# Local attention on one core: look-ahead of three items instead of two, a fourth buffer of v, and class-order copies on VectorE

## The chip, the core and the metric

The kernel runs on one core of a Trainium2 chip. A core has a matrix engine (TensorE, PE in the profile, with its weight loads apart as PEld), a vector engine (VectorE, DVE), a scalar engine (ScalarE, ACT), a general engine (GpSimd, POOL) and a queue engine that here only issues DMA transfers (SyncE, SP). Each engine takes its own instructions strictly in the order in which the program gives them, and waits on semaphores for the work of others. The metric is the device time of one launch in microseconds (us). PEclk in the profile is the clock granted to TensorE: 1.00 is 2.4 GHz and 0.50 is 1.2 GHz; a value between them is a stretch with some of each.

## The reference

Two blocks follow each other on 1024 tokens of width 1024. The first (gated linear attention, pooling, a mixture of experts) is not touched. The second computes a short gated convolution and eight heads of dilated local attention, and multiplies both by `w_out_2`. What matters here is the attention:

```python
DILATED_CONFIGS = ((128, 1), (512, 4), (2048, 16))      # (window, dilation)
q = rmsnorm_2(q.reshape(b, s, 8, 64), q_norm_w)
k = rmsnorm_2(k.reshape(b, s, 8, 64), k_norm_w)
for window, dilation in DILATED_CONFIGS:
    # queries and keys are split into `dilation` residue classes, swept in blocks of 128 queries
    logits = einsum('bhnqd,bhnkd->bhnqk', qr, kblk) * 64 ** -0.5
    logits = where(mask, logits + bias, -1e30)
    m = max(logits); p = exp(logits - m); denom = sum(p)
    o_i = einsum('bhnqk,bhnkd->bhnqd', p, vblk) / denom;  lse_i = m + log(denom)
mix = softmax(stack(lses), axis=0)
o = einsum('gbsh,gbshd->bshd', mix, stack(outs))
y_attn = o.reshape(b, s, 512) * silu(z_attn)
x = x + concatenate([y_conv, y_attn]) @ w_out
```

## The kernel before

The attention runs over four pairs of heads. A pair has 12 items: four of dilation 4 (configuration 1), four of dilation 16 (configuration 2), four of dilation 1 (configuration 0), in this order; `stream` lists the 48 items. One round of the loop at L1683 is a step g, and each engine gets its instructions in the order in which a step writes them:

- `load_values` of item g+2: SP issues the DMA of its block of v into a tile `vt` (L1454 to L1464, three buffers).
- `powers` of item g+2: TensorE makes the scores (L1500), VectorE adds the bias and takes the row's extreme value (L1506), ScalarE takes the exponential (L1508). The result is the tile `sb`.
- `turn_powers` of item g+1: TensorE transposes `sb` (L1526); the result is copied from PSUM to `pt`, one half by ScalarE (L1528), one by VectorE (L1530).
- `weigh` of item g: TensorE multiplies `pt` with `vt` (L1559), ScalarE copies the result to `og` (L1561, L1564 or L1566, by configuration).
- On some steps `next_part`: twelve matmuls of a product with `w_out_2` (L161 to L163), which needs nothing of the attention.
- `late.step()`: work put off by a number of steps. One such part is `mix_weights` (L1580 to L1594) and its `spread`: TensorE transposes the mixing weights (L1599), ScalarE copies them (L1601), SP writes them to DRAM as `sw_d` (L1603) and reads them back six times, broadcast (`zb`, L1607, 256 KB each). Another is `close_heads` (L1617 to L1621): POOL and VectorE multiply the three outputs of a pair by `zb` and add them. `ship_stats` sends row statistics to DRAM and back (`st_d`, L1574 to L1578).

Configurations 1 and 2 need queries and keys in class order. `by_class` makes these copies: `qd` and `kd` (L1487), 128x1024 fp32 each, read with steps of 4 or 8 elements (16 or 32 bytes). Configuration 2's are written behind the powers of item (1,1) of a pair, those of configuration 1 of the next pair behind the powers of item (0,1). A pair of numbers like (0,1) is configuration and item. So each pair has four copies, 16 in all; two are made before the loop.

Tiles come from pools of a fixed number of buffers: 26 of 4 KB under the name "blk" (`sb`, `pt`, `og`, `qd`, `kd`, `zb`, parts of `w_out_2`), six "tmp", four "wr" (raw weights), eight banks of PSUM.

Of the kernel before, what the change touches and what calls it, by code (L numbers as in the profile page):

```python
# [12 lines left out]
F32 = mybir.dt.float32  # L13
# [7 lines left out]
P = 128  # L21
# [44 lines left out]
def first_then_second_block(ctx: ExitStack, tc: tile.TileContext, a: dict, out: bass.AP):  # L66
    nc = tc.nc
    V, A, G, PE, SY = nc.vector, nc.scalar, nc.gpsimd, nc.tensor, nc.sync
# [7 lines left out]
    NTMP = 6  # L76
# [8 lines left out]
    def blk(name, shape=(P, 2, 512), dtype=F32):  # L85
        return B.tile(list(shape), dtype, name=name, tag="blk", bufs=NBLK)

    def psum(shape, name="ps"):
        t = PS.tile([P, 512], F32, name=name, tag="ps")
        n = int(np.prod(shape[1:]))  # L90
        v = t[: shape[0], :n]
        if len(shape) == 3:
            v = v.rearrange("p (a b) -> p a b", a=shape[1])
        elif len(shape) == 4:
            v = v.rearrange("p (a b c) -> p a b c", a=shape[1], b=shape[2])
        return v
# [194 lines left out]
    W = first.enter_context(tc.tile_pool(name="first", bufs=1))  # L291
# [836 lines left out]
    with tc.For_i(0, end_reg, 1):  # L1128
# [48 lines left out]
        for i, w in enumerate((wg, wu)):  # L1177
            src = w[bass.ds(e_reg, 1)].rearrange("o (p k) n -> p (o k) n", p=P)
# [15 lines left out]
        src = wd[bass.ds(e_reg, 1)].rearrange("o (p k) n -> p (o k) n", p=P)  # L1194
# [18 lines left out]
    W = att.enter_context(tc.tile_pool(name="attn", bufs=1))  # L1213
# [219 lines left out]
    hd = {}  # L1433
    def begin_heads(hp):
        s = hd[hp] = {}
        b14 = W.tile([P, 2, 2, 256], F32, name="b14", tag="b14", bufs=2)
        b16 = W.tile([P, 2, P], F32, name="b16", tag="b16", bufs=2)
        for h in range(2):
            for c in range(2):
                SY.dma_start(b14[:, c, h, :], dram_ap(skew_d, ((2 * hp + h) * 3 + c) * SKEW + P - 1, [[NSK - 1, P], [1, 256]]))  # L1440
            SY.dma_start(b16[:, h, :], dram_ap(skew_d, ((2 * hp + h) * 3 + 2) * SKEW + P - 1, [[NSK - 1, P], [1, P]]))
        s["bias"] = b14, b16
        s["tok"] = W.tile([P, 3, 8, 2, 2], F32, name="tok", tag="tok", bufs=2)
        s["st"] = [s["tok"][:, 0]] + [W.tile([P, 8, 2, 2], F32, name=f"st{c}", tag=f"st{c}", bufs=2) for c in (1, 2)]
        s["og"], s["sb"], s["pt"], s["v"] = {}, {}, {}, {}
        s["qk"] = {0: (qT[hp], kT[hp])}

    def load_values(hp, cfg, pr):
        c0 = hp * P
        v = hd[hp]["v"][cfg, pr] = W.tile([P, 3, P], F32, name="vt", tag="vt", bufs=3)  # L1450
        if cfg == 0:
            lo, hi = 256 * pr - 64, 256 * pr + 320
            if pr == 0:
                SY.dma_start(v[:64, 0, :], v_d[:64, c0:c0 + P])  # L1454
                lo += P
            if pr == 3:
                SY.dma_start(v[64:, 2, :], v_d[960:, c0:c0 + P])
                hi -= P
            k0 = (lo + 64 - 256 * pr) // P
            SY.dma_start(v[:, k0:k0 + (hi - lo) // P, :], v_d[lo:hi, c0:c0 + P].rearrange("(c p) n -> p c n", p=P))  # L1460
        elif cfg == 1:
            SY.dma_start(v[:, :2, :], v_d.rearrange("(b p r) n -> p b r n", p=P, r=4)[:, :, pr, c0:c0 + P])
        else:
            SY.dma_start(v[:, :2, :], v_d.rearrange("(p i) n -> p i n", i=8)[:, 2 * pr:2 * pr + 2, c0:c0 + P])  # L1464
# [17 lines left out]
    def by_class(hp, cfg):  # L1482
        n = DILS[1] if cfg == 1 else 8
        both = []
        for name, src in (("qd", qT[hp]), ("kd", kT[hp])):
            dst = blk(name, (P, n, T // n))
            G.tensor_copy(dst, src.rearrange("p (l r) -> p r l", r=n))  # L1487
            both.append(dst.rearrange("p r l -> p (r l)"))
        hd[hp]["qk"][cfg] = both

    def powers(hp, cfg, pr):
        s = hd[hp]
        qs, ks = s["qk"][cfg]
        b14, b16 = s["bias"]
        sp = [psum((P, 2, 256)) for _ in range(2)]
        sb = s["sb"][cfg, pr] = blk("sb")
        for i, (qc, kc, boff, n) in enumerate(units_of(cfg, pr)):
            for h in range(2):
                r = slice(64 * h, 64 * h + 64)
                PE.matmul(sp[h][:, i, :n], qs[r, qc], ks[r, kc], start=True, stop=True)  # L1500
        for i, (qc, kc, boff, n) in enumerate(units_of(cfg, pr)):
            for h in range(2):
                bias = b16[:, h, :] if cfg == 2 else b14[:, cfg, h, boff:boff + n]
                stat = s["st"][cfg][:, 2 * pr + i, h, :]
                p = sb[:, h, STEP[cfg] * i:STEP[cfg] * i + n]
                s_min = V.tensor_tensor_reduce(out=p, in0=sp[h][:, i, :n], in1=bias, scale=1.0, scalar=3.0e38,  # L1506
                                               op0=OP.add, op1=OP.min, accum_out=stat[:, 0:1])
                s_exp = A.activation(p, p, AF.Exp, bias=stat[:, 0:1], scale=-1.0, accum_out=stat[:, 1:2])  # L1508
                newest[:] = [s_min.ins, s_exp.ins]
# [70 lines left out]
    def mix_weights(hp):  # L1580
        s = hd[hp]
        tok = s["tok"]
        mn = W.tile([P, 8, 2], F32, name="mn", tag="mn", bufs=2)
        V.tensor_tensor(mn, tok[:, 0, :, :, 0], tok[:, 1, :, :, 0], op=OP.min)
        V.tensor_tensor(mn, mn, tok[:, 2, :, :, 0], op=OP.min)
        sg = W.tile([P, 3, 8, 2], F32, name="sg3", tag="sg3", bufs=2)
        V.tensor_sub(sg, mn[:, None].to_broadcast([P, 3, 8, 2]), tok[:, :, :, :, 0])
        A.activation(sg, sg, AF.Exp)
        zz = W.tile([P, 3, 8, 2], F32, name="zz", tag="zz", bufs=2)
        V.tensor_mul(zz, sg, tok[:, :, :, :, 1])  # L1590
        V.tensor_add(mn, zz[:, 0], zz[:, 1])
        V.tensor_add(mn, mn, zz[:, 2])
        V.reciprocal(mn, mn)
        sw = W.tile([P, 3, 2, 8], F32, name="sw", tag="sw", bufs=2)  # L1594
        V.tensor_mul(sw.rearrange("p c h b -> p c b h"), sg, mn[:, None].to_broadcast([P, 3, 8, 2]))

        def spread():
            ps = psum((48, P))
            PE.transpose(ps, sw.rearrange("p c h b -> p (c h b)"), ident)  # L1599
            swT = W.tile([48, P], F32, name="swT", tag="swT", bufs=1)  # L1600
            A.copy(swT, ps)  # L1601
            w_d = tc.dram_tile([6, T], F32, name=f"sw_d{hp}")
            SY.dma_start(w_d.rearrange("c (b p) -> (c b) p", p=P), swT)  # L1603
            s["zb"] = [blk("zb", (P, T)) for _ in range(3)]
            for cfg in range(3):
                for h in range(2):
                    SY.dma_start(s["zb"][cfg][64 * h:64 * h + 64, :], w_d[2 * cfg + h:2 * cfg + h + 1, :].to_broadcast([64, T]))  # L1607

        late.at(SPREAD, spread)
# [72 lines left out]

    stream = [(hp,) + it for hp in range(4) for it in items]  # L1683
    NS = len(stream)
    for g in range(-2, NS):
        if g + 2 < NS:
            hp, cfg, pr = stream[g + 2]
            if g == -2:
                begin_heads(hp)
                by_class(hp, cfg)  # L1690
            load_values(hp, cfg, pr)
            powers(hp, cfg, pr)
            if (cfg, pr) == (1, 1):
                by_class(hp, 2)
            elif (cfg, pr) == (0, 1) and hp < 3:
                begin_heads(hp + 1)
                by_class(hp + 1, 1)
            if cfg and pr == 3:
                late.at(2, lambda hp=hp, cfg=cfg: ship_stats(hp, cfg))
            if (cfg, pr) == items[-1]:  # L1700
                late.at(MIX, lambda hp=hp: mix_weights(hp))
        if 0 <= g + 1 < NS:
            turn_powers(*stream[g + 1])
        if g >= 0:
            weigh(*stream[g])
            if g % NI == NI - 1:
                late.at(CLOSE, lambda hp=stream[g][0]: behind(lambda: close_heads(hp)))
        if fill and g % GFILL == 0:
            fill.pop(0)()
        elif not fill and conv_part and g >= CBEG and (g - CBEG) % CSTEP == 0:  # L1710
            next_part()
        if g == CBEG - 3:
            prepare(*conv_part[0])
        if g == NS - EARLY:
            while conv_part:
                next_part()
            yT[0].clear()
            for kp in range(2, 4):
                load_out(0, kp)
        late.step()  # L1720
# [57 lines left out]
```

## Time and profile before

| | |
|---|---|
| median of three runs | 1626.17 us (1624.89 to 1628.64) |
| the profiled execution | 1627.21 us, of which the span that the profiler covers is 1625.5 us |
| TensorE busy over the span | 1535.9 us (94%) |
| VectorE, ScalarE, POOL busy | 1021.1, 801.2, 210.8 us |
| mean granted clock of TensorE | 0.972 |

The attention loop stands at about 1385 to 1566 us of the span. TensorE is busy for 164.1 of these 181 us; after the loop there is only the rest of the product with `w_out_2`, in which it does not wait. A row of a timeline reads: start, duration, engine, line, operation, output tile, input tiles, shape, and in brackets the idle time of that engine just before with what released it. A row of waits reads: engine, tile and line that waited, what it waited for, total, number of times, longest.

### The profile page before, as it was taken

How to read it: one execution, taken by the hardware profiler on the slowest of the kernel's cores; microseconds unless marked ns; L12 is line 12 of the kernel's file. 1: busy time of each engine (PE TensorE's matmuls, PEld its weight loads, DVE VectorE, ACT ScalarE, POOL GpSimd, SP SyncE). 2: the span in 40 equal slices, each digit the busy share in tenths (PEclk: the TensorE clock that was granted, in tenths of full speed). 3: DMA queues.
4: the chain of work that ended last, by engine and by line, in shares of the span. 5: the costliest groups of instructions: out<-in, count | busy, mean ns of one | idle time of the engine just before them, and what ended most of it. 6: DMA issues, size and time to landing. Idle time of an engine off the chain costs nothing. (4 is left out here: it accounts for less than half of the span.)

```text
span 1625.5 us, 24026 instructions
## 1 busy us (share of the span) xinstructions
PE 1535.9 (94%) x8678; PEld 1266.6 (78%) x8678; DVE 1021.1 (63%) x2278; ACT 801.2 (49%) x1635; POOL 210.8 (13%) x196
## 2 busy tenths in 40 slices
PE   7999999999999994999989897999999999999899
PEld 6888888887888874998888786888877787666667
DVE  5596444667644355998877686766655545676663
ACT  4434323453433232888777684524443326866550
POOL 1000000000000003232232111200000100243311
PEclk9999999999999996999999998999999999999999
DMA  6233334436323458999999996434423331445445
GB/s 193 65 82 106 103 109 163 136 115 195 104 80 115 142 215 281 295 270 319 328 312 335 296 335 194 156 102 164 149 88 104 104 103 41 120 119 147 103 137 169
DMA packets 168022, 272.01 MB, mean 167 GB/s; under 512 B 32689, under 2 KB 111932, under 8 KB 167773
## 3 DMA queue, kind: packets, MB, share of 16 engines
q1 hardware_dynamic: 154204, 232.13, 44.5%
q0 software_dynamic: 13680, 38.32, 8.5%
q8 instruction: 69, 1.13, 0.3%
q14 instruction: 53, 0.43, 0.1%
q10 hardware_dynamic: 16, 0.00, 0.0%
HBM read 243.92 MB, written 39.59 MB: 174 GB/s over the span
## 5 line engine op out<-in xcount | busy, mean ns | idle before, releaser
L127 ACT CAST wh<-wr 128x512 fp32r<-128x512 f32 (+1 forms) x248 | 170.6, 716 | 341.9 <-PE ps L162 192.5
L127 DVE TENSOR_TENSOR wl<-wr,wh 128x512 fp32r<-128x512 f32 (+1 forms) x248 | 202.3, 832 | 169.4 <-ACT wh L127 162.7
L127 DVE TENSOR_TENSOR wl<-ew,wh 128x1024 fp32r<-128x1024 f32 x144 | 172.6, 1220 | 44.3 <-ACT wh L127 43.6
L161 PE MATMUL ps<-h,wh 128*128 128x512 f32 x448 | 176.8, 395 | 0.0
L127 ACT CAST wh<-ew 128x1024 fp32r<-128x1024 f32 x144 | 149.7, 1052 | 54.4 <-PE ps L163 34.8
L163 PE MATMUL ps<-h,wl 128*128 128x512 f32 x448 | 175.3, 391 | 0.0
L162 PE MATMUL ps<-h,wh 128*128 128x512 f32 x448 | 175.3, 391 | 0.0
L161 PE MATMUL ps<-g,wh 128*128 128x512 f32 x320 | 126.1, 395 | 0.0
L162 PE MATMUL ps<-g,wh 128*128 128x512 f32 x320 | 125.2, 392 | 0.0
L163 PE MATMUL ps<-g,wl 128*128 128x512 f32 x320 | 124.8, 391 | 0.0
L161 PE MATMUL ps<-wh,xh 128*96 128x256 f32 x384 | 112.3, 293 | 6.2 <-ACT act L1023 6.2
L162 PE MATMUL ps<-wl,xh 128*96 128x256 f32 x384 | 110.9, 289 | 1.5 <-DVE wl L127 1.5
L163 PE MATMUL ps<-wh,xh 128*96 128x256 f32 x384 | 110.8, 289 | 0.0
L163 PEld LDWEIGHTS ps<-h,wl 128*128 128x128 f32 x448 | 84.6, 189 | 17.8
L161 PEld LDWEIGHTS ps<-h,wh 128*128 128x128 f32 x448 | 84.7, 189 | 17.5
L162 PEld LDWEIGHTS ps<-h,wh 128*128 128x128 f32 x448 | 84.6, 189 | 17.2
L985 POOL DMA_INDIRECT x_acc<-yt,row_idx x31 | 52.1, 1679 | 208.2 <-ACT yt L1045 147.6
L161 PE MATMUL ps<-wh,g 128*128 128x512 f32 x192 | 76.3, 398 | 0.0
L528 POOL DMA_DIRECT2D x_acc<-x x7 | 3.8, 536 | 551.7 <-DVE x L930 294.0
L163 PE MATMUL ps<-wh,g 128*128 128x512 f32 x192 | 75.1, 391 | 0.0
L162 PE MATMUL ps<-wl,g 128*128 128x512 f32 x192 | 74.9, 390 | 0.0
L161 PEld LDWEIGHTS ps<-wh,xh 128*96 128x96 f32 x384 | 65.8, 171 | 8.2 <-ACT act L1023 7.0
(455 smaller groups left out, 3642.0 us busy)
## 6 DMA issues: line engine op xcount, KB each, us to landing
wr<-in_w_in_dram SPq DMA_DIRECT2D x128, 512.0 KB, 3.9
ew<-in_w_exp_down_dram SPq DMA_DIRECT2D x64, 512.0 KB, 9.7
ew<-in_w_exp_gate_dram SPq DMA_DIRECT2D x64, 512.0 KB, 8.0
ew<-in_w_exp_up_dram SPq DMA_DIRECT2D x64, 512.0 KB, 9.5
wr<-in_w_out_dram SPq DMA_DIRECT2D x24, 512.0 KB, 3.9
xs<-xb_rows POOLq DMA_DIRECT2D x28, 256.0 KB, 3.3
x<-in_x_dram SPq DMA_DIRECT2D x12, 512.0 KB, 6.3
zb<-sw_d SPq DMA_DIRECT2D x24, 256.0 KB, 5.2
```

The lines of the kernel that those rows point to most:

```text
L127: both = A.copy(hi, src), V.tensor_sub(lo, src, hi.bitcast(F32))
L161: PE.matmul(ps, lhs[0], rhs[0], start=start, stop=False)
L162: PE.matmul(ps, lhs[0], rhs[1], start=False, stop=False)
L163: PE.matmul(ps, lhs[1], rhs[0], start=False, stop=stop)
L528: G.dma_start(x_acc[t * P:(t + 1) * P], x1)
L985: G.indirect_dma_start(out=x_acc, out_offset=bass.IndirectOffsetOnAxis(ap=idx[:n], axis=0), in_=src[:n], in_offset=None, bounds_check=T - ...
```

## The change

`LEAD` is 3, so that `load_values` and `powers` run three items ahead of `weigh` rather than two; `turn_powers` stays one item ahead. `vt` has four buffers rather than three. The copies of L1487 move from GpSimd (`G`) to VectorE (`V`). `swT` takes a buffer of "tmp" rather than one of its own. The whole diff (V is VectorE, G is GpSimd, W the pool of tiles):

```diff
-        v = hd[hp]["v"][cfg, pr] = W.tile([P, 3, P], F32, name="vt", tag="vt", bufs=3)
+        v = hd[hp]["v"][cfg, pr] = W.tile([P, 3, P], F32, name="vt", tag="vt", bufs=4)
...
-            G.tensor_copy(dst, src.rearrange("p (l r) -> p r l", r=n))
+            V.tensor_copy(dst, src.rearrange("p (l r) -> p r l", r=n))
...
-            swT = W.tile([48, P], F32, name="swT", tag="swT", bufs=1)
+            swT = W.tile([P, 512], F32, name="swT", tag="tmp", bufs=NTMP)[:48, :P]
...
-    for g in range(-2, NS):
-        if g + 2 < NS:
-            hp, cfg, pr = stream[g + 2]
-            if g == -2:
+    LEAD = 3
+    for g in range(-LEAD, NS):
+        if g + LEAD < NS:
+            hp, cfg, pr = stream[g + LEAD]
+            if g == -LEAD:
```

The lines behind these move by one. Lines and shapes in the rows below are the kernel's; + stands for the changed kernel, - for the one before.

On VectorE, in the second pair at the powers of its item (0,1), the copies for the third pair now stand between the row extremes of item (0,1) (L1506) and the copy of a `pt` (L1530):

```order
 L1506 ISA sb,tok<-ps,b_12771 128x256
 L1506 ISA tok 128x1
+L1487 COPY qd<-qT_9910 128x1024
+L1487 COPY kd<-kT_9906 128x1024
+L1530 COPY pt<-ps 128x256
+L1506 ISA sb,tok<-ps,b_12771 128x256
+L1506 ISA tok 128x1
```

The `pt` copy that follows them belongs to item (2,3), which is two items behind (0,1) in the stream; in the kernel before, POOL made the two copies and they stood in no row of VectorE.

On TensorE, at the same place of the first pair:

```order
 L1559 MATMUL ps<-pt,vt 64x128 x4
 L1500 MATMUL ps<-kT_9905,qT_9909 128x256 x4
-L1526 MATMUL ps<-ident,sb 128x128 x8
+L1526 MATMUL ps<-ident,sb 128x128 x4
 L1559 MATMUL ps<-pt,vt 64x128 x4
 L1500 MATMUL ps<-kT_9905,qT_9909 128x256 x4
 L1526 MATMUL ps<-ident,sb 128x128 x8
-L1559 MATMUL ps<-pt,vt 64x128 x8
+L1559 MATMUL ps<-pt,vt 64x128 x4
```

Behind the scores of item (0,1) (the first L1500) there now follow the transposes of (2,3) rather than of (0,0), the products of (2,2), the scores of (0,2), the transposes of (0,0), and the products of (2,3): transposes and products belong to items one further behind the scores.

On SP, around the transfers of the first pair's mixing weights, before:

```order
-L1603 DMA sw_d_13512<-swT 48x128
-L1462 DMA vt<-v_rows 128x2x128
-L1607 DMA zb<-sw_d_13512 64x1024 x6
-L1574 DMA st_d_1_13661<-st_13265 512x1x4 x2
-L1464 DMA vt<-v_rows 128x2x128
-L1578 DMA tok<-st_d_1_13661 128x8x4
```

and now:

```order
+L1603 DMA sw_d_13491<-swT 48x128
+L1657 DMA xb_rows<-xs 128x512
+L1607 DMA zb<-sw_d_13491 64x1024 x6
+L1462 DMA vt<-v_rows 128x2x128
+L1464 DMA vt<-v_rows 128x2x128
+L1574 DMA st_d_1_13638<-st_13250 512x1x4 x2
+L1464 DMA vt<-v_rows 128x2x128
```

The loads of v for items (1,3) (L1462) and (2,0) (the first L1464) now follow the six `zb` at once, ahead of the two `st_d`, and item (1,3) is itself now behind the `zb`.

## Rows read from the trace of the kernel before

**Rows 1.** The page, busy time by engine over the whole span.
```profile
PE 1535.9 (94%) x8678; PEld 1266.6 (78%) x8678; DVE 1021.1 (63%) x2278; ACT 801.2 (49%) x1635; POOL 210.8 (13%) x196
```

**Rows 2.** Waits between 1385 and 1570 us.
```profile
PE ps L1526 <- ACT sb L1508: 9.1, 8, 2.7
...
PE ps L1559 <- DMA vt<-v_rows: 6.3, 3, 2.7
```

**Rows 3.** TensorE's timeline, the rows with waits of 1 us and more (four of seven).
```profile
1431.02 0.66 PE L1559 MATMUL ps<-pt,vt 128*64 128x128 f32 x8 [1.08 <-DMA vt<-v_rows]
...
1439.54 1.25 PE L1526 MATMUL ps<-ident,sb 128*128 128x128 f32 x3 [2.12 <-ACT sb L1508]
...
1509.95 0.44 PE L1526 MATMUL ps<-ident,sb 128*128 128x128 f32 x2 [2.71 <-ACT sb L1508]
1538.03 0.90 PE L1559 MATMUL ps<-pt,vt 128*64 128x128 f32 x8 [2.71 <-DMA vt<-v_rows]
```

**Rows 4.** Windows of 2 us: busy time by engine, then granted clock, DMA share, GB/s.
```profile
1424.00:1426.00 2.00, 2.00 (x23) 1.58 (x22) 1.86 (x10) 0.89 (x5) 0.00 (x0) 1.00 1.06 244
1432.00:1434.00 2.00, 2.00 (x10) 1.64 (x9) 1.43 (x1) 0.47 (x1) 2.00 (x2) 1.00 0.77 178
1538.00:1540.00 2.00, 1.97 (x11) 1.48 (x12) 0.40 (x1) 0.63 (x1) 2.00 (x2) 0.58 0.53 103
1540.00:1542.00 2.00, 2.00 (x7) 1.57 (x6) 1.20 (x1) 0.00 (x0) 2.00 (x3) 0.57 0.79 231
```

**Rows 5.** Timelines of TensorE and SP around the second pair's start, and the critical chain.
```profile
1414.68 0.29 PE L1599 MATMUL ps<-ident,sw 128*48 128x128 f32 x1
...
1418.63 4.06 SPq L1607 DMA_DIRECT2D zb<-sw_d  x6
1422.73 1.28 SPq L1574 DMA_DIRECT2D st_d<-st  x2
1424.11 0.57 SPq L1464 DMA_DIRECT2D vt<-v_rows  x1
...
1424.11 6.78 DMA vt<-v_rows
```

**Rows 6.** Timelines of VectorE and POOL at the third pair's end.
```profile
1503.96 4.95 DVE L127 TENSOR_TENSOR wl<-wr,wh 128x1024 fp32r<-128x1024 f32 x1
...
1503.78 2.08 POOL L1487 COPY qd<-qT 128x1024 f32<-128x1024 f32 x1
```

**Rows 7.** Groups by shape: busy, mean ns, idle (L1487, L1530: 1385 to 1570).
```profile
L1487 POOL COPY qd<-qT 128x1024 f32<-128x1024 f32 x6 | 12.5, 2080 | 7.1 <-PE ps L1559 7.1
L127 DVE TENSOR_TENSOR wl<-ew,wh 128x1024 fp32r<-128x1024 f32 x144 | 172.6, 1220 | 44.3 <-ACT wh L127 43.6
L1245 DVE TENSOR_SCALAR u<-u,rsq_y 128x1024 f32<-128x1024 f32 x4 | 2.8, 744 | 0.0
L1530 DVE COPY pt<-ps 128x256 f32<-128x256 f32 x16 | 6.7, 418 | 2.2 <-PE ps L1526 2.2
```

**Rows 8.** VectorE's timeline, four row extremes of one item.
```profile
1395.52 0.42 DVE L1506 CUSTOM_DVE_ANT_0 sb<-ps,b 128x256 f32<-128x256 f32 x1 [0.97 <-PE ps L1500]
...
1396.90 0.69 DVE L1530 COPY pt<-ps 128x512 f32<-128x512 f32 x1
```

**Rows 9.** The critical chain, one step of configuration 0, and one matmul of `next_part`.
```profile
1394.43 1.06 PE ps L1500 x8
1395.49 1.02 PE ps L1526 x8
1396.51 0.61 PE ps L1559 x8
...
1421.82 0.23 PE ps L163
```

**Rows 10.** POOL's timeline, closing the first pair (two calls of two products).
```profile
1426.02 2.50 POOL L1617 TENSOR_TENSOR og<-og,zb 128x512 f32<-128x512 f32 x2 [10.28 <-DMA zb<-sw_d]
1429.90 2.97 POOL L1617 TENSOR_TENSOR og<-og,zb 128x512 f32<-128x512 f32 x2 [1.39 <-ACT og L1564]
```

## The prediction

> **What bounds the kernel now.** I read the page first: TensorE is busy for 94% of the span, VectorE for 63% [rows 1]. So what a change can give back is TensorE's idle time and the time in which its clock is low. The waits of the attention loop name both kinds: 9.1 us in eight waits of the transposes (L1526) for an exponential (L1508), and 6.3 us in three waits of the weighted sums (L1559) for a block of v [rows 2]. TensorE's timeline says where: the waits for v come once at the start of the second, third and fourth pair, when the previous pair's weights are broadcast (1.08 us at 1431, 2.71 at 1538, and one between them, which by the total of rows 2 took 2.5); the largest waits for exponentials are the 2.12 us at 1439.54, where VectorE closes a pair, and the 2.71 us at 1509.95, at the third pair's end [rows 3]. Then the windows of the granted clock: after the 1.08 us it stays at 1.00, after the 2.71 us at 1538 it stands at 0.58 and 0.57 for two windows with TensorE busy nearly throughout [rows 4]. Two microseconds at 0.57 do the work of 1.15, so the two windows lose 0.42 x 2 + 0.43 x 2 = 1.7 us. The waits of 2.5 and of 2.71 (at 1510) are as long, and I charge each with as much: an idle stretch of some 2.5 us cost about 4.4 us here, one of 1 us cost 1.
>
> All sums are changes to the profiled execution of 1627.2 us, which is 1.0 us above the median of the runs, 1626.2; I carry them to the median. What the measurement can tell from no change is about 0.2%, 3.3 us.
>
> **The change part by part.**
>
> *Loads of v.* In the second pair SP issues six broadcasts from 1418.63 to 1422.69, then two `st_d` (1.28 us), and only then the load of v that TensorE waits for at 1430; it is taken up 6.78 us after its issue at 1424.11 [rows 5]. Counted from the transpose of the mixing weights at 1414.68, the load is issued at +9.4 and there at +16.2, while TensorE wants it at 1431.02 - 1.08 = 1429.94, +15.3 [rows 3, 5]. With three items ahead, the loads for (1,3) and (2,0) stand directly behind the broadcasts, and the mixing weights come a step earlier too, so that the load one item before now takes the critical place, wanted at about the same +15.3 to +15.5. It gains the 1.28 us of the two `st_d`. So each wait shrinks by 1.3: 1.08 to 0, 2.5 to about 1.1, 2.71 to about 1.3; with 0.1 less for the later need, 6.3 becomes 2.3, a gain of **4.0**. Bounds: nothing, if the broadcasts' data and not the issue sets the arrival (rival 1 below), to all 6.3. The fourth buffer of `vt` is what lets the load be issued three items ahead; it adds no work.
>
> *POOL's copies gone.* At the third pair's end VectorE's split of `w_out_2` (L127 `wl`), started at 1503.96, took 4.95 us, and ran beside POOL's copies `qd` and `kd`, the first begun at 1503.78 [rows 6]; 144 instructions of the same form and size took 1.22 on average [rows 7]. The row extremes behind it came 3.7 us late, and TensorE waited 2.71 at 1510 for their exponentials [rows 3]. Without POOL's copies this instruction takes its 1.22: a gain of **2.7**. Bounds: nothing, if as long a wait comes behind VectorE's own copies (priced below), to 2.7.
>
> *One item more between scores and transposes.* At 1439.54 VectorE's closing work kept the row extremes of an item waiting until TensorE stood 2.12 us [rows 3]. With one more item in hand it should be less, but the copies of `pt` (L1530) stand behind the same work in VectorE's order and are not a step further ahead. I take **0.5** off, between nothing and 2.1.
>
> *Clock.* If the waits of 2.5, 2.71 and 2.71 fall to about 1.1, 1.3 and 0, they are of the size of the 1.08 that left the clock at 1.00 [rows 4]: a gain of 3 x 1.7 = **5.1**. Bounds: nothing to that. What the clock loses behind the 2.12 us wait I leave where it is.
>
> *Copies on VectorE.* 14 of 16 lie in the loop. No row shows VectorE copying with steps of 16 or 32 bytes. From below: a one-source instruction over 128x1024 without steps took 0.744 us; from above: POOL's copy with the same steps took 2.08 [rows 7]. I take 1.2 us each, the duration of VectorE's two-source instruction of this size, which goes at one element per step [rows 7]. TensorE's work hides some of it. At the three places where the next pair's copies are made, VectorE must finish, after the scores of (0,1), four row extremes (1.38 us from the first's start to the start behind the last, [rows 8], 1.47 with the handover), two copies c, and the `pt` copy of (2,3), 0.42 [rows 7], with 0.1 of handover: 2.0 + 2c. TensorE meanwhile has the transposes of (2,3) and the products of (2,2), about 0.6 each, the scores of (0,2), 1.06, and the transposes of (0,0), 1.02 [rows 9]: 3.3, and 0.1 for handover. It waits 2c - 1.4: 1.0 at c = 1.2, three times: a cost of **3.0**. At 0.744 it is 0.3, at 2.08 it is 8.3. At the four other places, behind (1,1), a `next_part` stands in between, twelve matmuls of 0.23 us [rows 9], 2.8 in all: 2c - 4.2 is nothing up to c = 2.1. Without that cover they would cost as much as the others.
>
> The Trainium skill ("SBUF — State Buffer", section "Specifications (TRN2)") speaks against this part: SBUF is read in lines of 16 bytes, full bandwidth wants at least two hits in a line, and each step to a new line pays a penalty. With steps of 16 and 32 bytes every element lies in a line of its own. The trace has no VectorE row for it; POOL's copies agree as far as they go, at 2.08 us for 1024 elements. By the rule the time would go towards rival 2's 1627.3, by the 1.2 taken above it is 1617.
>
> *`swT` in the "tmp" pool.* It waits for a buffer whose earlier user is a delivered `xs`, long gone; the copy itself is unchanged. Nothing, and if a buffer were late, SP's broadcasts would be.
>
> Sum: -4.0 - 2.7 - 0.5 - 5.1 + 3.0 = **-9.3**, from 1627.2 to 1617.9, and 1616.9, rounded **1617**, on the scale of the median.
>
> **The rivals.**
>
> 1. *v still waits.* While the broadcasts run, the DMA engines are full (share 1.06 at 1424 to 1426, [rows 4]); if the data ahead, not SP's issue, set the arrival, the 4.0 and the clock behind the two longer waits (3.4) do not come. That is -1.9, **1624.3**. For it: the full engines. Against: `st_d` is issued ahead of it, and 1.28 us are SP's own.
> 2. *Slow copies.* At 2.08 us the three waits are 2.8 each, long enough for the clock to fall behind each: 8.3 + 5.1 in place of 3.0, **1627.3**, no change. It needs c above 1.9. The rule of the Trainium skill quoted above would act this way.
> 3. *Everything is hidden.* Copies at 0.744 us (0.3 in place of 3.0), v in time (2.3 more): **1611.9**.
> 4. *Slower: buffers run short.* One more item ahead keeps one more `sb` alive in the pool of 26. If the `pt` of an early item of a pair then gets its buffer from the close of the pair before, TensorE waits for POOL, which multiplies only after the broadcasts: its first two products are done at 1426.02 + 2.50, +13.8 from the transpose of the weights, the second two at 1429.90 + 2.97, +18.2 [rows 5, 10]. The first is in time for a need at about +15.4, the second 2.8 too late; three times that and the clock with it is 8.4 + 5.1, **1630.4**. It decides from 2.9 us of wait a pair on.
>
> **How the numbers follow.** My forecast 0.50; rival 1 0.15; rival 2 0.10; rival 3 0.14; rival 4 0.11. Faster by over 0.2% (below 1622.9): forecast, rival 3 and a part of rival 1, whose term of 4.0 may come in part: 0.70. Within 0.2%: the rest of rival 1, and rival 2: 0.17. Slower: rival 4 and copies beyond 2.1 us: 0.13. The range must take in rivals 1 to 3 and leaves out rival 4: 1610 to 1628; the forecast's own is 1613 to 1621.
>
> **What would show it.** After: `wl` at the third pair's end at 1.2 us; L1487 on VectorE between 0.74 and 2.1 us, which decides the copies; waits of L1559 for v of 2.3 us in all, at the starts of the pairs; new waits of about 1 us at L1559 for the `pt` copy of (2,3), at three places; the granted clock at 1.00 at the starts of the pairs and at 0.5 only behind the closing of a pair. I am wrong if L1487 takes 2 us or more, if the waits for v stay at 6, if POOL's L1617 releases a `pt`, or if the largest wait for exponentials is as long as before at another place.

## The result

The changed kernel takes 1605.85 us in the median of four runs (1603.39 to 1612.38), the kernel before 1626.02 beside it (1624.89 to 1628.64). The ratio is 0.988, with a 95% interval of 0.9845 to 0.9915. So it is faster, as forecast, but by 20.2 us where 9.3 were forecast, and the time lies below the range of 1610 to 1628.

The profiled execution took 1603.39 us, the fastest of the four and 23.8 less than the one of before. Of that, 4.6 us lie ahead of the attention and are not the change's: TensorE's first scores begin at 1348.64 us where they began at 1353.22, and over the kernels below, which are the same up to there, they begin anywhere from 1349 to 1357. I therefore measure the change on what I call the **stretch**: from TensorE's first scores (L1500) to its first matmul on the attention's own `yT` (L161, a row that ends a wait for ScalarE). It is 1566.11 - 1353.22 = 212.9 us before and 1542.25 - 1348.64 = 193.6 after: **-19.3 us**. Behind it both kernels need 59.4 us.

The 19.3 us split into two sums and a rest. The waits that the timeline shows in the stretch fall from 16.3 to 6.4 us (-9.9). The clock, summed over windows of 2 us as 2 x (1 - granted clock), costs 8.5 before and 3.4 after (-5.1). The remaining 4.2 us are in neither sum. First the waits of the changed kernel, as a total and then on TensorE's timeline; they answer to [rows 2, 3]:

```profile
PE ps L1559 <- ACT pt L1528: 4.7, 3, 3.0
...
PEld ps L1526 <- ACT sb L1508: 2.1, 7, 0.3
...
PE ps L1559 <- DVE pt L1530: 0.7, 2, 0.4
```

```profile
1393.15 0.65 PE L1559 MATMUL ps<-pt,vt 128*64 128x128 f32 x6 [0.31 <-DVE pt L1530]
...
1400.23 1.09 PE L1559 MATMUL ps<-pt,vt 128*64 128x128 f32 x16 [1.40 <-ACT pt L1528]
...
1435.74 0.65 PE L1559 MATMUL ps<-pt,vt 128*64 128x128 f32 x6 [0.38 <-DVE pt L1530]
...
1531.63 2.17 PE L1559 MATMUL ps<-pt,vt 64*64 64x128 f32 x16 [3.01 <-ACT pt L1528]
...
1542.25 0.50 PE L161 MATMUL ps<-wh,yT 128*128 128x512 f32 x1 [0.99 <-ACT yT L127]
```

No wait of the transposes (L1526) for an exponential is left, and no wait for v. What is left stands at the weighted sums, for a `pt`: 0.3 to 0.4 us where VectorE makes class-order copies, and 3.01 at the end of the fourth pair, behind which the clock is at its lower level, 1.2 GHz, for three windows:

```profile
1530.00:1532.00 2.00, 0.37 (x4) 0.29 (x4) 2.00 (x10) 2.00 (x9) 0.54 (x1) 0.80 1.07 387
1532.00:1534.00 2.00, 2.00 (x18) 1.42 (x15) 0.69 (x4) 2.00 (x10) 0.00 (x0) 0.50 0.97 352
...
1536.00:1538.00 2.00, 2.00 (x18) 1.67 (x15) 1.38 (x6) 0.35 (x1) 0.00 (x0) 0.50 0.00 0
```

I take the 4.2 us outside both sums for waits too short to be printed as idle time of the matmuls; that is argued, since the 4.2 are only what the two sums leave. Such waits show in the weight loads, which come before the matmuls. Before, the transposes' weight loads waited 19.0 us, in 38 waits, for exponentials, and the eight waits of 9.1 us [rows 2] are the long ones among them. After, they wait 2.1 us in seven (the row above), and 3.2 us for VectorE (L1656, L1530, L1506) have come. The kernel before:

```profile
PEld ps L1526 <- ACT sb L1508: 19.0, 38, 3.0
...
1418.45 0.76 PE L1526 MATMUL ps<-ident,sb 128*128 128x128 f32 x2
```

Two transposes take 0.76 us there; the same two take 0.44 where nothing holds them [rows 3]. Such a row reads as busy.

Next the close of the first pair, at which TensorE waited 2.12 us for an exponential before [rows 3]. VectorE and POOL in the changed kernel:

```profile
1425.68 1.28 DVE L1617 TENSOR_TENSOR og<-og,zb 128x512 f32<-128x512 f32 x2
1426.89 1.28 DVE L1619 TENSOR_TENSOR og<-og 128x512 f32<-128x512 f32 x2
...
1429.89 0.35 DVE L1506 CUSTOM_DVE_ANT_0 sb<-ps,b 128x192 f32<-128x192 f32 x1
...
1416.49 2.55 POOL L1617 TENSOR_TENSOR og<-og,zb 128x512 f32<-128x512 f32 x2 [36.65 <-ACT sb L1508]
1419.25 2.51 POOL L1617 TENSOR_TENSOR og<-og,zb 128x512 f32<-128x512 f32 x2 [0.22 <-DMA zb<-sw_d]
1421.72 2.50 POOL L1618 TENSOR_TENSOR og<-og 128x512 f32<-128x512 f32 x2
```

and in the kernel before:

```profile
1430.58 2.85 DVE L1617 TENSOR_TENSOR og<-og,zb 128x512 f32<-128x512 f32 x2
1434.61 2.34 DVE L1619 TENSOR_TENSOR og<-og 128x512 f32<-128x512 f32 x2 [1.18 <-POOL og L1618]
...
1438.67 0.28 DVE L1506 CUSTOM_DVE_ANT_0 sb<-ps,b 128x128 f32<-128x128 f32 x1
```

Before, VectorE's close overlapped POOL's [rows 10], waited for it and ran slowly: 8.1 us from its first product to the next row extremes (1438.67 - 1430.58). After, the mixing weights come a step earlier: from their transpose (L1599) to VectorE's first product it is 18.6 us (1425.68 - 1407.05) instead of 15.9 (1430.58 - 1414.68), and to POOL's 9.4 instead of 11.3. POOL is through at 1424.2, before VectorE begins, and VectorE needs 4.2 us (1429.89 - 1425.68). A `next_part` of 2.8 us on TensorE stands beside the close in both kernels; it covers most of the 4.2 us, but not of the 8.1.

Last the class-order copies on VectorE, and the product behind them:

```profile
1433.21 1.11 DVE L1487 COPY qd<-qT 128x1024 f32<-128x1024 f32 x1
1434.25 1.11 DVE L1487 COPY kd<-kT 128x1024 f32<-128x1024 f32 x1
1435.29 0.40 DVE L1530 COPY pt<-ps 128x256 f32<-128x256 f32 x1
...
L1487 DVE COPY qd<-qT 128x1024 f32<-128x1024 f32 x8 | 9.1, 1140 | 0.0
```

They take 1.14 us each. TensorE waits 0.38 us for the `pt` copy behind them (its row at 1435.74 above).

### The profile page after: what moved, and what is told of

Its sections match the earlier page's. It is cut to its first block, busy times and chain, and to the rows that moved or that the text cites. A ratio compares the mean times of both kernels' runs of the same rounds, so it can differ in the third digit from the quotient of the medians.

```text
span 1601.7 us, 23955 instructions
## 1 busy us (share of the span) xinstructions
PE 1521.9 (95%) x8678; PEld 1260.3 (79%) x8678; DVE 1021.9 (64%) x2294; ACT 800.7 (50%) x1635; POOL 173.6 (11%) x180
## 5 line engine op out<-in xcount | busy, mean ns | idle before, releaser
L127 ACT CAST wh<-wr 128x512 fp32r<-128x512 f32 (+1 forms) x248 | 170.6, 716 | 340.9 <-PE ps L162 192.6
L127 DVE TENSOR_TENSOR wl<-wr,wh 128x512 fp32r<-128x512 f32 (+1 forms) x248 | 196.0, 807 | 166.8 <-ACT wh L127 160.0
L127 DVE TENSOR_TENSOR wl<-ew,wh 128x1024 fp32r<-128x1024 f32 x144 | 172.8, 1220 | 42.9 <-ACT wh L127 41.8
L161 PE MATMUL ps<-h,wh 128*128 128x512 f32 x448 | 176.5, 394 | 0.0
L127 ACT CAST wh<-ew 128x1024 fp32r<-128x1024 f32 x144 | 149.8, 1051 | 51.8 <-PE ps L163 33.3
L161 PE MATMUL ps<-g,wh 128*128 128x512 f32 x320 | 125.5, 393 | 0.0
L161 PE MATMUL ps<-wh,xh 128*96 128x256 f32 x384 | 113.2, 295 | 10.8 <-ACT act L1023 10.8
L161 PEld LDWEIGHTS ps<-h,wh 128*128 128x128 f32 x448 | 84.6, 189 | 17.6
L161 PE MATMUL ps<-wh,g 128*128 128x512 f32 x192 | 76.3, 398 | 0.0
L161 PEld LDWEIGHTS ps<-wh,xh 128*96 128x96 f32 x384 | 66.1, 172 | 12.8 <-ACT act L1023 11.6
L161 PEld LDWEIGHTS ps<-g,wh 128*128 128x128 f32 x320 | 60.1, 188 | 13.0 <-issue 0.6
```

The source lines that it names most:

```text
L127: both = A.copy(hi, src), V.tensor_sub(lo, src, hi.bitcast(F32))
L161: PE.matmul(ps, lhs[0], rhs[0], start=start, stop=False)
```

## The experiments

Each run is compared with the kernel before on the same chip. Stretch, waits and clock are those of one profiled execution. "Waits" are those shown on TensorE's timeline in the stretch, "clock" is the sum over 2 us windows as above.

| kernel | median us | ratio to before (95%) | stretch | waits | clock |
|---|---|---|---|---|---|
| before | 1626.0 | | 212.9 | 16.3 | 8.5 |
| copies alone (`copies_only`) | 1622.95 | 0.9965 (0.995 to 0.9981) | 208.7 | 13.0 | 6.9 |
| loads of v alone (`v_only`) | 1636.8 | 1.0042 (1.0024 to 1.006) | 221.2 | 23.0 | 15.4 |
| powers alone (`powers_only`) | 1626.99 | 0.9987 (0.9969 to 1.0004) | 212.0 | 16.8 | 11.9 |
| loads and powers (`lead_only`) | 1619.74 | 0.9945 (0.9927 to 0.9963) | 205.4 | 15.3 | 5.1 |
| loads and copies (`v_copies`) | 1627.48 | 0.9987 (0.9972 to 1.0002) | 213.3 | 16.5 | 10.2 |
| powers and copies (`powers_copies`) | 1614.2 | 0.9906 (0.9878 to 0.9934) | 200.2 | 11.2 | 5.1 |
| all (the change) | 1605.85 | 0.988 (0.9845 to 0.9915) | 193.6 | 6.4 | 3.4 |
| all, again (`after_again`) | 1607.43 | 0.9862 (0.9835 to 0.9888) | 189.6 | 5.2 | 0.0 |

The first theory to test was that the look-ahead is nearly all of the gain; its rival, that the gain that was not forecast comes from POOL's copies being gone.

**Look-ahead without the copies' move**, `lead_only`:

```diff
-            V.tensor_copy(dst, src.rearrange("p (l r) -> p r l", r=n))
+            G.tensor_copy(dst, src.rearrange("p (l r) -> p r l", r=n))
```

> The change with the class-order copies left on POOL. The attention stretch (TensorE's first scores to the end of its wait for the first attention yT) was 212.9 us before and 193.6 after. Look-ahead theory: nearly all of the gain is here, stretch 194 to 199 us, time 1604 to 1612; VectorE's instruction beside POOL's copies may still take 4 to 5 us, but TensorE does not wait for it. Copies theory (the gain that was not forecast comes from POOL's copies being gone): stretch 204 to 208, time 1615 to 1620.

It measured 205.4: the look-ahead theory missed by more than 6 us, and stretch and time (1619.74 us) lie in the range of the copies theory. The copies stand behind POOL's closing products here, and fall on VectorE's close (VectorE, POOL and TensorE):

```profile
1428.43 3.44 DVE L1617 TENSOR_TENSOR og<-og,zb 128x512 f32<-128x512 f32 x2
1431.80 3.13 DVE L1619 TENSOR_TENSOR og<-og 128x512 f32<-128x512 f32 x2
...
1428.86 2.47 POOL L1487 COPY qd<-qT 128x1024 f32<-128x1024 f32 x1
1431.26 2.51 POOL L1487 COPY kd<-kT 128x1024 f32<-128x1024 f32 x1
...
1436.18 0.66 PE L1526 MATMUL ps<-ident,sb 128*128 128x128 f32 x4 [1.74 <-DVE xs L1656]
...
1500.89 1.98 PE L1559 MATMUL ps<-pt,vt 128*64 128x128 f32 x16 [4.25 <-ACT pt L1528]
```

Two pairs of VectorE instructions that take 1.28 us in the changed kernel take 3.44 and 3.13. The 4.25 us at the third pair's end have another cause, which neither theory named: ScalarE stands for 5.17 us at a split of `w_out_2` whose load was issued at 1489.93. That is 32.5 us behind the transpose of the second pair's mixing weights; in the changed kernel it is 26.4 (1477.48 - 1451.12). Why SP comes to it later I did not pursue.

**The copies' move alone**, `copies_only` (the change's second line of the diff on the kernel before):

> Only the class-order copies move to VectorE; two items ahead and three buffers of v as before. Look-ahead theory: the 2.71 us wait at the third pair's end and its half clock go (4.4 us), the v waits of 6.3 us stay, and the copies of 1.14 us each delay exponentials that have no slack: stretch 207 to 213 us, time 1620 to 1627. Copies theory: stretch 199 to 204, time 1611 to 1617.

208.7, in the look-ahead theory's range and over the copies theory's 199 to 204. So neither theory holds in both runs. The `wl` at the third pair's end (L127) is at 1.22 us without POOL's copies beside it, and the wait of 2.71 us behind it is gone. A wait of 1.71 us for v is left at the first close (the same products of the next two pairs wait 1.52 and 1.67, which the profile puts down to an exponential), and 2.33 for an exponential at the second close:

```profile
1432.64 0.66 PE L1559 MATMUL ps<-pt,vt 128*64 128x128 f32 x8 [1.71 <-DMA vt<-v_rows]
...
1489.61 1.10 PE L1526 MATMUL ps<-ident,sb 128*128 128x128 f32 x3 [2.33 <-ACT sb L1508]
```

**Loads of v alone**, `v_only`: the kernel before with four buffers, `swT` in the "tmp" pool, and

```diff
-            load_values(hp, cfg, pr)
+                load_values(hp, cfg, pr)
+            if g + 3 < NS:
+                load_values(*stream[g + 3])
```

> Only the loads of v run three items ahead, with four buffers; powers two items ahead, copies on POOL. Loads theory (v in time is worth what it cost, 6.3 us of waits and two half clocks of 1.7): stretch about 203 us, time 1616. Look-ahead theory: at most that, since the waits of the transposes for exponentials (9.1 us shown and the short ones) stay, and TensorE reaches the next one sooner: stretch 203 to 209, time 1616 to 1622.

A miss for both, in sign: 8.3 us longer. All 6.3 us of waits for v are gone, and there are 17.8 us of waits at the three closes, where the first close had 2.12 before (TensorE and VectorE, first close):

```profile
1444.99 1.24 PE L1526 MATMUL ps<-ident,sb 128*128 128x128 f32 x3 [7.21 <-ACT sb L1508]
...
1436.45 4.15 DVE L1619 TENSOR_TENSOR og<-og 128x512 f32<-128x512 f32 x2 [1.16 <-POOL og L1618]
```

Removing a wait brought TensorE earlier to the close, where the next transposes need exponentials that VectorE holds up; POOL's copies, 1437.60 to 1442.5, make that longer. A wait that is taken away alone is not worth its length.

**Powers alone**, `powers_only`: `LEAD` 3, but `load_values` for item g+2 and three buffers, copies on POOL.

> Only the powers run three items ahead; loads of v two items ahead in three buffers, copies on POOL. Look-ahead theory: waits of transposes for exponentials fall from 9.1 us to under 2, the weight loads' waits for exponentials from 19 us to under 4, while waits for v stay at 4 to 8 us with a half clock behind two of them: stretch 200 to 206 us, time 1612 to 1619. Loads theory: stretch within 3 us of 212.9.

212.0, where 200 to 206 was expected and the rival's 3 us holds. The transposes' waits for exponentials have gone as expected. Waits for v stay, at 4.1 us; beside them stand 12.7 us of other waits, among them 3.01 us behind VectorE beside POOL's copies, and 11.9 of clock (TensorE and, second, VectorE):

```profile
1453.56 1.11 PE L1526 MATMUL ps<-ident,sb 128*128 128x128 f32 x4 [3.01 <-DVE st L1506]
...
1447.89 4.42 DVE L1584 TENSOR_TENSOR mn<-tok 128x16 f32<-128x16 f32 x1
...
1476.98 1.76 PE L1559 MATMUL ps<-pt,vt 128*64 128x128 f32 x16 [2.30 <-DMA vt<-v_rows]
```

The 4.42 us are those of an instruction over 128x16, which takes 0.17 us in the changed kernel; POOL's two copies lie beside it, from 1448.26 to 1452.26, and it ends at 1452.31.

After these four both first theories were dropped: alone, the three parts move the stretch by -4.1, +8.3 and -0.9 us, together by -19.3. The next runs take them two at a time.

**Loads and copies**, `v_copies`:

> Loads of v three items ahead with four buffers and copies on VectorE; powers two items ahead. The loads alone gave a stretch of 221.2 us, worse than the 212.9 of before, with 17.8 us of waits where VectorE closes a pair; POOL's copies ran beside VectorE's products there. POOL theory (those waits come from POOL's copies holding VectorE): the close's waits fall to about 3 us in all, stretch 198 to 204, time 1611 to 1617. Rival (the waits come because an item that is not delayed by v meets the close with no slack in the powers): waits of 10 us and more at the close stay, stretch 208 to 216, time 1620 to 1629.

213.3: the rival is right. With POOL's copies gone the closes still hold 11.2 us of waits, instead of 17.8:

```profile
1547.04 1.24 PE L1526 MATMUL ps<-ident,sb 128*128 128x128 f32 x3 [4.20 <-ACT sb L1508]
```

So 6.6 of the 17.8 us were POOL's. I put most of the rest down to a lack of slack between the scores and the transposes: with the powers three items ahead and all else the same (the change), no wait of the transposes is left.

**Powers and copies**, `powers_copies`:

> Powers three items ahead and copies on VectorE; loads of v two items ahead in three buffers. If loads of v matter once the rest is in place, waits for v of 4 to 6 us with half clocks of 1.7 to 3.4 us behind them stay: stretch 200 to 206 us, time 1613 to 1619. If the two other parts are all of it: stretch 193 to 197, time 1604 to 1609.

200.2: loads of v matter once the rest is in place. 5.4 us of waits for v are left, one a pair, and one of them has a half clock behind it:

```profile
1427.77 1.04 PE L1559 MATMUL ps<-pt,vt 128*64 128x128 f32 x16 [2.19 <-DMA vt<-v_rows]
```

**POOL's copies beside the rest**, `pool_copies_too`: the changed kernel with

```diff
+            spare = W.tile([P, n // 2, T // n], F32, name="spare", tag="tmp", bufs=NTMP)
+            for i in range(2):
+                G.tensor_copy(spare, src.rearrange("p (l r) -> p r l", r=n)[:, n // 2 * i:n // 2 * (i + 1)])
```

> The changed kernel, in which POOL makes the class-order copies as well, at the same places, into a spare buffer that nobody reads (a tile of the tmp pool, in two halves). Theory that POOL's reading of SBUF slows VectorE's two-source instructions: VectorE's products at a pair's close (L1617, L1619) take 1.0 to 1.2 us on average where the changed kernel has 0.69 and 0.82, waits for exponentials and pt copies come back at the closes, stretch 198 to 206 us, time 1612 to 1620. Rival (in the kernels with POOL's copies it was the scores' wait for the copies themselves that cost): VectorE slower, but the stretch within 3 us of the changed kernel's 189.6 to 193.6.

1608.66 us, ratio 0.9875 (0.9853 to 0.9897), stretch 193.0. It did not test what it was meant for: into a "tmp" buffer the copies ran ahead of POOL's close, from 1415.58 on, not beside VectorE's, and VectorE's products stayed at 0.69 us each:

```profile
1415.58 1.12 POOL L1490 COPY spare<-qT 128x512 f32<-128x512 f32 x1
...
L1620 DVE TENSOR_TENSOR og<-og,zb 128x512 f32<-128x512 f32 x10 | 6.4, 686 | 1.8 <-DMA zb<-sw_d 1.8
```

It shows that POOL's copies cost nothing measurable where they fall beside nothing that they hold: the stretch lies between the changed kernel's two (193.6 and, below, 189.6). So they were put where they had fallen in `lead_only`.

**POOL's copies at the close**, `pool_at_close`: the changed kernel with, behind L1618,

```diff
+            spare = W.tile([P, 4, P], F32, name="spare", tag="tmp", bufs=NTMP)
+            for i in range(2):
+                G.tensor_copy(spare, og[1][:, sl].rearrange("p (l r) -> p r l", r=4))
```

> The changed kernel, in which POOL also makes four copies of 128x512 with steps of 16 bytes behind its own sum (L1618) at each pair's close, into a spare buffer that nobody reads, so that they stand beside VectorE's closing products and sums; nothing waits for them. Theory that a POOL instruction that reads SBUF holds up VectorE's instructions with two SBUF sources: VectorE's two products and two sums at the first three closes take 2 us and more for a pair of them where the changed kernel has 1.28, the close grows by 2 to 4 us, and waits of 1 to 2 us for exponentials or pt copies come back at each of the three closes: stretch 193 to 202 us, time 1608 to 1616. Rival (it is POOL's queue, not its reading): VectorE's durations stay at 1.28, stretch 189 to 194.

1610.5 us, ratio 0.9882 (0.9858 to 0.9906), stretch 196.4 where the changed kernel has 189.6 with as short a wait at its end (1.36 and 1.33 us). The timelines of POOL and VectorE, and the group of VectorE's products:

```profile
1425.02 5.20 POOL L1621 COPY spare<-og 128x512 f32<-128x512 f32 x4
...
1426.37 2.88 DVE L1617 TENSOR_TENSOR og<-og,zb 128x512 f32<-128x512 f32 x2
1429.18 2.19 DVE L1622 TENSOR_TENSOR og<-og 128x512 f32<-128x512 f32 x2
...
L1617 DVE TENSOR_TENSOR og<-og,zb 128x512 f32<-128x512 f32 x10 | 11.1, 1152 | 1.0 <-DMA zb<-sw_d 1.0
```

No instruction waits for these copies, nor does VectorE wait at the closes for the loads of `xs` that stand behind them in POOL's order. Still VectorE's two pairs take 2.88 and 2.19 us where they took 1.28 each; TensorE's waits come back at all three closes, 1.1 to 2.1 us each, and 1.7 us of clock. So it is POOL's instruction itself that holds VectorE up; whether by its reading or its writing was not tried. In the stretch that is 6.8 us, between one execution of each; in the time the two are not told apart (0.9882 against 0.988 and 0.9862). The Trainium skill ("SBUF — State Buffer", section "Who interferes with whom") says that a VectorE instruction with two SBUF inputs contends with a GpSimd instruction that reads SBUF; the 2.88 against 1.28 agrees, and so do the 4.95 against 1.22 of [rows 6, 7].

**Three buffers of v**, `vt3`:

```diff
-        v = hd[hp]["v"][cfg, pr] = W.tile([P, 3, P], F32, name="vt", tag="vt", bufs=4)
+        v = hd[hp]["v"][cfg, pr] = W.tile([P, 3, P], F32, name="vt", tag="vt", bufs=3)
```

> The changed kernel with three buffers of v. The load three items ahead then waits on SP for the products of the item before, so that it is issued no earlier than two items ahead, and SP's queue stands behind it: waits for v of 4 to 6 us come back, stretch 197 to 202 us as with loads two items ahead (200.2), time 1611 to 1616. Rival (the fourth buffer is only room): stretch 189 to 194.

1610.17 us, ratio 0.9887 (0.9866 to 0.9908), stretch 194.1: near the rival. Waits for v come back, but 0.8 us in all, so the fourth buffer is worth little. `powers_copies`, which has three buffers too but issues the loads an item later, kept 5.4 us of them: most of the gain is the place of the load in SP's order.

```profile
1427.66 1.04 PE L1559 MATMUL ps<-pt,vt 128*64 128x128 f32 x16 [0.47 <-DMA vt<-v_rows]
```

**Powers four ahead**, `lead4` (`LEAD = 4`, `load_values` of item g+3):

> Powers four items ahead, loads of v three items ahead in four buffers, all else as in the changed kernel. If three items take all that can be had, the waits left (1.4 us at the first pair's end, 1.3 to 3.0 at the last, 0.3 at the copies) are not waits for exponentials of late items: stretch 188 to 195 us, within 3 us of the changed kernel. Rival (one more item hides them too): stretch 186 to 188. Other rival (one item more runs the pool of 26 short): waits for a pt or sb buffer, stretch over 197.

1611.56 us, ratio 0.9904 (0.9884 to 0.9924), no faster than three. The stretch, which here ends without the last wait, is 197.1 us: the rival of a pool run short is nearest. Waits of 0.8 to 1.3 us for a `pt` have come back at the ends of pairs; whether buffers cause them was not tried.

```profile
1499.63 0.55 PE L1559 MATMUL ps<-pt,vt 128*64 128x128 f32 x6 [1.29 <-ACT pt L1528]
```

**A later split of the last weights**, `late_split`, and the changed kernel beside it, `after_again`:

```diff
+    behind(lambda: [turn_weights(0, kp) for kp in range(2, 4)])
     for t in range(4):
         open_ps[t] = psum((P, 512))
```

> The changed kernel, with the split of the last two loads of w_out_2 (L127) written behind the last powers, so that ScalarE does not wait for their transfer ahead of exponentials. The changed kernel's one long wait, 3.0 us at the fourth pair's end, and the 3.4 us that half clock costs behind it go: stretch 187 to 189 us, time 5 to 6 us under the changed kernel. Rival (the split is then late for the first product that uses it, or the wait moves to the end of the stretch): stretch 191 to 195, no faster than the changed kernel.

> The changed kernel again, beside the others on one chip: stretch 193 to 194 us and about 19 us under the kernel before, 1605 to 1610 us.

1604.8 us, ratio 0.9844 (0.9818 to 0.987), against 1607.43 and 0.9862 (0.9835 to 0.9888): the two are not told apart. In the profiled execution of `late_split`, the slowest of its five at 1609.65, the wait is gone from the stretch (189.2 us), but the wait for the last `yT` doubled to 1.94, the clock is at 0.50 from 1546 to 1552 behind it, and the rest of the kernel took 61.7 us where it takes 59.4. And in `after_again` itself the wait that the edit was to remove was short, without a half clock, with nothing changed:

```profile
1546.21 0.79 PE L161 MATMUL ps<-wh,yT 128*128 128x512 f32 x1 [1.94 <-ACT yT L127]
```

```profile
1534.18 1.24 PE L1559 MATMUL ps<-pt,vt 64*64 64x128 f32 x16 [1.33 <-ACT pt L1528]
```

The first row is of `late_split`, the second of `after_again`. The stretch of `after_again` is 189.6 us, where 193 to 194 was expected. ScalarE waits 2.92 us there for a load of `w_out_2` (L127) for which it waited 4.61 in the first execution. So most of the 4.1 us between the two stretches (193.6 and 189.6) go with one late load of weights and the clock behind it, with the same program.

## Why the prediction was wrong

The direction and most of the places were right; the size failed at one step, and the way of summing separate terms is refuted by the runs.

*The step that failed* is "One item more between scores and transposes", priced at 0.5 us because "the copies of `pt` (L1530) stand behind the same work in VectorE's order and are not a step further ahead". The copies of `pt` are no further ahead, but they did not bind: at the first close the `pt` copy stands ahead of the close, at 1425.35, and the next is made at 1431.13, while a `next_part`, scores and earlier transposes keep TensorE busy from 1425.47 on. What is gone is all 9.1 us of waits for exponentials [rows 2], of which only the 2.71 stood in the sum beside this term, and with them most of the short waits that the weight loads' row shows (19.0 us in 38 waits), a row that the prediction did not read. Of the 9.1, the 2.71 was rightly put to POOL's copies; against the rest waits of 1.40 and 3.01 us for ScalarE's `pt` have come. Of the 10.0 us that the sum of 9.3 lacks in the stretch, loads of v make 2.3 (6.3 for 4.0), the copies' waits 2.0 (1.0 for 3.0), the clock nothing, and the other 5.7 fall to this term: some 6 us, the 4.2 of short waits in it, where 0.5 stood. Alone the term gains 0.9 (`powers_only`), with the others in place 20 to 24: `v_copies`, without it, has a stretch of 213.3, the change 193.6 and 189.6.

*The sum of separate terms.* Loads of v were priced at 4.0, POOL's copies at 2.7, and the clock at 5.1, each on the waits of before. Alone, the loads cost 8.3 us and the powers' look-ahead gains 0.9; powers and copies gain 12.7 together. A wait taken away lets TensorE reach the next late item sooner; it pays only where that item is ready.

*Loads of v*: priced 4.0 with bounds 0 to 6.3; all 6.3 are gone. In the change SP begins the broadcasts at +2.0 from the transpose of the weights (1409.07 - 1407.05), where it began them at +3.95 [rows 5], so that the two loads behind them go out at +5.7 and +6.8, not at +8.1 as reckoned (9.4 - 1.3). TensorE and SP of the changed kernel:

```profile
1407.05 0.27 PE L1599 MATMUL ps<-ident,sw 128*48 128x128 f32 x1
...
1409.07 3.65 SPq L1607 DMA_DIRECT2D zb<-sw_d  x6
1412.77 0.59 SPq L1462 DMA_DIRECT2D vt<-v_rows  x1
1413.84 0.37 SPq L1464 DMA_DIRECT2D vt<-v_rows  x1
```

The broadcasts' earlier start, 1.9 us that the forecast did not have, is about what makes the difference. Rival 1, that the data ahead in the full DMA engines set the arrival, did not come: the change has no wait for v at all.

*POOL's copies gone*: right in mechanism and size at the place named (`wl` at 1.22 us in the change; the 2.71 gone, and gone in `copies_only`). Not seen was that with the look-ahead they would fall on the pair's close, as in `lead_only`. Keeping POOL clear of it is, as I read the runs, why copies and look-ahead gain more together.

*Clock*: 5.1 forecast, 5.1 measured in the profiled execution (8.5 to 3.4); that the two agree is luck. The three places named are gone, as forecast. But the half clock behind the close, which I "leave where it is" and which cost 3.4 us before, is gone too, and 3.4 us behind the new wait at 1531.63 have come; in the second execution all 8.5 are gone.

*Copies on VectorE*: 1.2 us taken, 1.14 measured. Their wait is 0.3 to 0.4 at each of the three places, not 1.0: the sum of 3.0 is 1.0 (at the third place, 1479.39, the 0.33 is put down to ScalarE's half of `pt`, and the products behind it are some 0.4 longer than elsewhere). The formula let the products of (2,3) start with VectorE's half of `pt`; two of eight rows of them stand ahead on ScalarE's half (0.43 us at 1434.93). The Trainium skill's rule on lines of 16 bytes ("SBUF — State Buffer", "Specifications (TRN2)") made the forecast wary of slow copies. The trace agrees as far as it goes: 1.14 us with these steps against 0.744 for another one-source instruction without steps [rows 7], and far from POOL's 2.08.

Rivals 2 (slow copies) and 4 (buffers) did not come. Rival 3, everything hidden, was nearest, but its 1611.9 was still made of the same terms.

Open: why SP's load of `w_out_2` comes later in `lead_only`, what holds `lead4`, and whether the 4.2 us outside the two sums are all short waits, and at which places.

## What to carry to other kernels

Read the weight loads' waits as well as the matmuls': a row of matmuls that looks busy can hold many waits of 0.3 us; here one step more of look-ahead removed most of them at once. Don't price the parts of a change one by one on the waits of the old trace when each shields the same engine; ask for each what TensorE meets next when that wait is gone, because a lone fix can cost time. And look where an engine's moved work falls beside the others': POOL's copies cost nothing measurable away from the closes and 6.8 us of the stretch at them.

## What the runs showed of the hardware

POOL copies hold up VectorE instructions that read two SBUF tiles, with no semaphore between them: 1.28 us became 2.88 in `pool_at_close` and 3.44 in `lead_only`. A short one can be held as long: one of 0.17 us took 4.42 in `powers_only`, until two POOL copies were through. The length of a wait alone did not tell what the clock does. In `powers_copies` the clock stayed at 1.00 behind the wait of 2.19 us that ended at 1427.77, and fell to 0.64 behind one of 1.80 us that ended at 1473.80 (and to 0.51, close to its lower level of 1.2 GHz, in the window after); windows of that run:

```profile
1428.00:1430.00 2.00, 2.00 (x30) 1.37 (x26) 0.52 (x5) 0.81 (x3) 2.00 (x3) 1.00 0.08 2
...
1474.00:1476.00 2.00, 2.00 (x24) 1.37 (x20) 0.00 (x0) 0.62 (x2) 2.00 (x2) 0.64 0.00 0
```
